# First mixer of a two-block kernel: queries projected ahead of the recurrence, near scores on row halves, modulation weights loaded in halves

## The chip, the cores and the metric

The kernel runs on one core of one Trainium2 chip. The number that counts is the device time of one execution in microseconds (us), lower is better. The engines that matter here are TensorE (PE), which multiplies matrices and loads its weights beside that (PEld); VectorE (DVE) and ScalarE (ACT), which work on elements; GpSimd (POOL); and SyncE (SP), whose queue issues the DMA transfers.

## The reference

Two transformer-like blocks, one after the other. The first has two layers, each with a mixer and a feed-forward part; every layer first turns the condition vectors into modulation rows (shift, scale, gate). This case touches only the first layer's mixer ("even mixer") and two thirds of that layer's modulation.

```python
m_lat = split((silu(c) @ mod_w[layer] + mod_b[layer]), 6)      # 1024 x 6144 weight, 2 rows (c, c_ctx)
h_lat = modulate(rms_norm(x), m_lat[0], m_lat[1])              # 512 tokens; h_ctx: 256 tokens
p  = split_parts(h_lat @ w_in)     # a_q 512, a_k 128, a_v 128, b_q, b_ff, b_fb, b_i, b_g 512 each
# attention: 8 query heads of 64 in 2 key heads; a 128-block sees its neighbours (window 128),
#            all 256 context keys and a sink column
q_lat = apply_rope(rms_norm(a_q));  k_lat = apply_rope(rms_norm(a_k))
s_lat = where(|k_pos - q_pos| <= 128, q_lat . k_lat * 64**-0.5, -inf);  s_ctx = q_lat . k_ctx * 64**-0.5
a_lat = softmax([sink, s_lat, s_ctx]) @ [v_lat, v_ctx]
# recurrence: 4 heads of 128, forward and backward, in chunks of 64, context first, then latent tokens
b_lat = rms_norm(gla(b_q, b_ff, b_i) + flip(gla(flip ...))) * silu(b_g)
y = concat(a_lat, b_lat) @ w_out                               # the same for the context tokens
```

## The kernel before

Tokens lie in columns, features in partitions: 512 latent and 256 context tokens, so one projection onto 128 features is done for 768 columns. Every weight matrix is loaded in float32 into a staging buffer `wr` (two buffers), split into a high part `wh` (ACT) and the rest `wl` (POOL) by `wsplit`, and used in three matmuls per 128 rows (`gemm`, L168 to L170): 8 x 3 matmuls of 128x512 (`hH`, `hL`, latent) and 8 x 3 of 128x256 (`cH`, `cL`, context). One projection is thus 48 matmuls, two PSUM tiles of the pool `mm`, which has two. Everything else that goes through PSUM in the mixer shares five banks with the tag `sm`.

`even_mixer` (its loop starts at `for hd in range(4)`) does four heads. Each head has, in this order in the code: the projections `wf`, `wb` (decays of the two directions), `wq`, `wg` (query and gate), the recurrence `hgrn_head`, which is a context part and then a latent part (each: scans and exponentials on DVE and ACT, transposes of `hkn` at L762, small matmuls at L778 to L812, a norm that ends in the matmul with `ones` at L823), then the attention queries' projection, their norm and rope (`qk_norm`, L627 to L635) and six attention blocks (`attend`: four latent blocks and two of context, scores at L649 and L652, transposes, values, and the last transposes at L701). PE fills what one head leaves open with projections of the next.

The order on each engine is not the order of the code: the tile framework sorts instructions by priority as they become ready and by the buffers that are free, once, at build time. On the chip each engine runs its list in that order.

Modulation of the layer is computed beside all this. Part 0 of its columns is done before the mixer; parts 1 and 2 (2048 columns each) are in a background list `bg` of Python generators, and `tick(1)` advances it by one step. A step is one row block of 128: a 1 MB load into the shared `wr` (L281), four matmuls of 32 columns each into column groups of one `sm` bank (L284), and an addition into `mrow` (L288, L290). In `two` (which does one projection) it is called as

```python
                self.later(100, self.tick, 1)
```

so it comes 100 priority steps behind the projection. Two matmul rows make one float32 matmul in the profile.

The keys of attention stand in two tiles `ak0`, `ak1` of 128 x 768. In each, one half of the partitions (64 rows, one key head) holds keys, and the other is zero, so that a product with the full 128-row query tile gives one key head's scores.

Of the kernel before, what the change touches and what calls it, by code (L numbers as in the profile page):

```python
# [67 lines left out]
class Core:  # L68
# [196 lines left out]
    def matvec(self, ps, sb, i0, w, c0, ncol, bias, dst, tag="mv"):  # L265


        nc, cond = self.nc, self.cond
        nj = ncol // 512
        np_ = 32 * nj  # L270
        rows = self.T(sb, [P, 512], "mrow")
        per = 2048 // ncol
        whole = tag == "mv"
        acc = None
        for k0 in range(0, KT, per):
            first, last = not whole or k0 == 0, not whole or k0 + per == KT
            if first:
                acc = self.T(ps, [P, 512], tag)
            r = self.wt("wr", [P, 2048])
            rv = r.rearrange("p (k c) -> p k c", k=per)  # L280
            nc.sync.dma_start(rv, w[k0 * P:(k0 + per) * P, c0:c0 + ncol].rearrange("(k p) c -> p k c", p=P))  # L281
            for kk in range(per):
                for j in range(nj):
                    nc.tensor.matmul(acc[32 * j:32 * j + 32, :], cond[:, k0 + kk, :], rv[:, kk, j * 512:(j + 1) * 512],  # L284
                                     start=(first and kk == 0), stop=(last and kk == per - 1), skip_group_check=True)
            if whole or k0 == 0:
                if last:
                    nc.vector.tensor_copy(rows[:np_, :], acc[:np_, :])  # L288
            else:
                nc.vector.tensor_tensor(rows[:np_, :], rows[:np_, :], acc[:np_, :], ALU.add)  # L290
            yield
        self.mv_out(ps, rows, nj, i0, 2, bias, dst, tag)

# [272 lines left out]
class Even(Core):  # L566
# [70 lines left out]
    def attend(self, ps, sb, q, k, vt, t, i, yq):  # L637
# [192 lines left out]
    def even_mixer(self, groups, ydram, side, mid, out):  # L830
# [3 lines left out]
        with tc.tile_pool(name="ev", bufs=1, reuse_waits="tile") as sb, tc.tile_pool(name="evmm", bufs=2, space=PSUM, reuse_waits="tile") as pm, \  # L834
# [33 lines left out]
            kr = self.T(sb, [P, TOK], "aq")  # L868
            self.qk_norm(ps, sb, pl, pc, self.qkg[:, 1:2], kr)

            k = [self.T(sb, [P, TOK], f"ak{i}") for i in range(2)]
            for i in range(2):
                rs, rz = slice(i * 64, i * 64 + 64), slice(64 - i * 64, 128 - i * 64)
                nc.gpsimd.memset(k[i][rz, :], 0.0)
                nc.gpsimd.tensor_copy(k[i][rs, :], kr[rs, :])
# [20 lines left out]
            for hd in range(4):  # L896
# [20 lines left out]

                r = self.wt("wr", [P, 2048])[:, :1024]
                rv = r.rearrange("p (k c) -> p k c", k=KT)
                for kv in range(2):  # L920
                    c = kv * 256 + hd * 64
                    nc.sync.dma_start(rv[:, :, kv * 64:(kv + 1) * 64], w[:, c:c + 64].rearrange("(k p) c -> p k c", p=P))
                H, L = self.wsplit(r)
                if hd == 3:
                    mid()
                pl, pc = two((H.rearrange("p (k c) -> p k c", k=KT), L.rearrange("p (k c) -> p k c", k=KT)))
                aq = self.T(sb, [P, TOK], "aq")
                self.qk_norm(ps, sb, pl, pc, self.qkg[:, 0:1], aq)
                yq = self.T(sb, [P, TOK], "yq", bufs=2)
                for i in range(6):  # L930
                    self.attend(ps, sb, aq, k, vt, hd, i, yq)
# [817 lines left out]
class Kernel(Second):  # L1749
    def run(self, out):  # L1750
# [13 lines left out]
        def matvecs(ps, sb, l, parts, tag="mv"):  # L1764
            for i in parts:
                c = slice(i * 16, i * 16 + 16)
                self.bg.append(self.matvec(ps, sb, 0, a["mod_w"][l], i * 2048, 2048,
                                           self.mb[:, l * 48 + i * 16:l * 48 + i * 16 + 16], self.modT[l][:, c, :], tag))
# [17 lines left out]
        with tc.tile_pool(name="x0", bufs=1, reuse_waits="tile") as xp, tc.tile_pool(name="n0", bufs=1, reuse_waits="tile") as sb, \  # L1786
# [9 lines left out]
            matvecs(*side(st, "mva"), 0, [0])  # L1796
# [26 lines left out]
        self.even_mixer(groups, yd, lambda ps, sb: matvecs(ps, sb, 0, [1, 2], "sm"), load_x, out_a)  # L1823
# [111 lines left out]
```

## Time and profile before

| what | us |
|---|---|
| time, median of 3 runs | 2943.16 (2942.12 to 2946.09) |
| time of the profiled execution | 2955.79 |
| its span in the trace | 2954.0 |
| PE busy in it | 2786.1 (94%) |
| DVE, ACT, POOL busy | 1396.0, 1064.5, 990.9 |
| mean granted TensorE clock | 0.972 of full speed |
| the four heads in the span | 127.6 to 610.6 |

The profiled execution is 12.6 us longer than the median of the timed runs. Positions below are microseconds from the start of the profiled span. The four heads take 16% of it. A head is read from its last attention transposes (L701) to those of the head before: 143.2, 116.1, 118.6 and 105.1 us.

### The profile page before, as it was taken

How to read it: one execution, taken by the hardware profiler on the slowest of the kernel's cores; microseconds unless marked ns; L12 is line 12 of the kernel's file. 1: busy time of each engine (PE TensorE's matmuls, PEld its weight loads, DVE VectorE, ACT ScalarE, POOL GpSimd, SP SyncE). 2: the span in 40 equal slices, each digit the busy share in tenths (PEclk: the TensorE clock that was granted, in tenths of full speed). 3: DMA queues.
4: the chain of work that ended last, by engine and by line, in shares of the span. 5: the costliest groups of instructions: out<-in, count | busy, mean ns of one | idle time of the engine just before them, and what ended most of it. 6: DMA issues, size and time to landing. Idle time of an engine off the chain costs nothing. (4 is left out here: it accounts for less than half of the span.)

```text
span 2954.0 us, 38203 instructions
## 1 busy us (share of the span) xinstructions
PE 2786.1 (94%) x15432; PEld 2301.8 (78%) x15432; DVE 1396.0 (47%) x2291; ACT 1064.5 (36%) x1964; POOL 990.9 (34%) x512
## 2 busy tenths in 40 slices
PE   5988989799999999999999999999999999999898
PEld 3866767678888888788888878877878788787677
DVE  5255655656645353633232326453363453542545
ACT  4234435433112112323233334222244444544533
POOL 2321212133223223234252435444434341332443
PEclk7999999999999999999999999999999999999999
DMA  6222121333323241122121214443124542443522
GB/s 258 72 84 85 49 84 54 97 106 117 106 106 127 82 157 40 54 71 85 57 86 57 72 47 168 161 151 101 57 98 139 159 147 74 126 131 128 191 77 86
DMA packets 216216, 306.39 MB, mean 104 GB/s; under 512 B 26918, under 2 KB 169800, under 8 KB 209512
## 3 DMA queue, kind: packets, MB, share of 16 engines
q1 hardware_dynamic: 216040, 303.96, 31.0%
q8 instruction: 121, 1.98, 0.3%
q14 instruction: 55, 0.45, 0.0%
HBM read 272.17 MB, written 31.75 MB: 103 GB/s over the span
## 5 line engine op out<-in xcount | busy, mean ns | idle before, releaser
L162 POOL TENSOR_TENSOR wl<-wr,wh 128x1024 fp32r<-128x1024 f32 x200 | 490.2, 2453 | 978.5 <-ACT wh L161 952.1
L168 PE MATMUL mm<-hH,wh 128*128 128x512 f32 (+1 forms) x1776 | 710.1, 401 | 13.3 <-ACT hH L189 5.0
L169 PE MATMUL mm<-hL,wh 128*128 128x512 f32 (+1 forms) x1776 | 707.8, 399 | 8.9 <-POOL hL L403 6.1
L170 PE MATMUL mm<-hH,wl 128*128 128x512 f32 (+1 forms) x1776 | 704.9, 397 | 2.5 <-POOL wl L162 2.5
L168 PEld LDWEIGHTS mm<-hH,wh 128*128 128x128 f32 x1776 | 338.5, 191 | 90.5 <-issue 7.2
L169 PEld LDWEIGHTS mm<-hL,wh 128*128 128x128 f32 x1776 | 339.0, 191 | 86.4 <-POOL hL L403 8.9
L161 ACT ACTIVATE wh<-wr 128x1024 fp32r<-128x1024 f32 x200 | 211.7, 1060 | 526.0 <-PE mm L169 427.0
L170 PEld LDWEIGHTS mm<-hH,wl 128*128 128x128 f32 x1776 | 339.3, 191 | 73.4 <-issue 3.7
L148 POOL TENSOR_TENSOR wl<-wr,wh 128x1024 fp32r<-128x1024 f32 x96 | 237.8, 2480 | 397.8 <-ACT wh L147 395.8
L416 DVE SCALAR_TENSOR_TENSOR x<-mm,modT,x 128x512 f32<-128x512 f32 (+1 forms) x340 | 213.9, 648 | 278.8 <-PE mm L170 276.4
L168 PE MATMUL mm<-aH,wh 128*128 128x512 f32 (+1 forms) x544 | 191.8, 354 | 3.0 <-DVE x L416 2.6
L169 PE MATMUL mm<-aL,wh 128*128 128x512 f32 (+1 forms) x544 | 191.0, 352 | 1.1 <-DVE aL L190 1.1
L170 PE MATMUL mm<-aH,wl 128*128 128x512 f32 (+1 forms) x544 | 191.7, 353 | 0.0
L168 PE MATMUL mm<-cH,wh 128*128 128x256 f32 x640 | 184.5, 288 | 6.5 <-DVE nt L398 6.3
L169 PE MATMUL mm<-cL,wh 128*128 128x256 f32 x640 | 185.0, 289 | 0.0
L170 PE MATMUL mm<-cH,wl 128*128 128x256 f32 x640 | 183.8, 287 | 0.0
L147 ACT ACTIVATE wh<-wr 128x1024 fp32r<-128x1024 f32 x96 | 101.1, 1055 | 165.7 <-PE mm L169 99.7
L168 PEld LDWEIGHTS mm<-cH,wh 128*128 128x128 f32 x640 | 123.4, 193 | 10.7 <-ACT cH L402 6.7
L169 PEld LDWEIGHTS mm<-cL,wh 128*128 128x128 f32 x640 | 123.4, 193 | 6.8 <-issue 4.4
L170 PEld LDWEIGHTS mm<-cH,wl 128*128 128x128 f32 x640 | 123.5, 193 | 2.8 <-issue 2.5
L190 DVE TENSOR_TENSOR aL<-sg,aH 128x512 fp32r<-128x512 f32 (+1 forms) x66 | 104.4, 1582 | 36.6 <-ACT aH L189 36.6
L314 DVE SCALAR_TENSOR_TENSOR macc<-wr,cond,macc 128x1024 f32<-128x1024 f32 (+1 forms) x56 | 109.8, 1979 | 18.6 <-DMA wr<-in_mod_w_dram 11.9
(504 smaller groups left out, 5060.5 us busy)
## 6 DMA issues: line engine op xcount, KB each, us to landing
wr<-in_mod_w_dram SPq DMA_DIRECT2D x48, 1024.0 KB, 5.3
wr<-in_ffn_w_in_dram SPq DMA_DIRECT2D x44, 1024.0 KB, 5.1
wr<-in_w_in_dram SPq DMA_DIRECT2D x36, 1024.0 KB, 5.4
wr<-in_odd_w_in_dram SPq DMA_DIRECT2D x24, 1024.0 KB, 5.1
wr<-in_ffn_w_out_dram SPq DMA_DIRECT2D x22, 1024.0 KB, 6.0
wr<-in_ada_w_dram SPq DMA_DIRECT2D x12, 1024.0 KB, 6.8
wr<-in_even_w_in_dram SPq DMA_DIRECT2D x18, 512.0 KB, 4.5
wr<-in_odd_w_out_dram SPq DMA_DIRECT2D x8, 1024.0 KB
```

The lines of the kernel that those rows point to most:

```text
L147: self.nc.scalar.activation(H, rv, AF.Copy)
L148: self.nc.gpsimd.tensor_tensor(L, rv, f32(H), ALU.subtract)
L161: self.nc.scalar.activation(H, v, AF.Copy)
L162: (engs[j] if engs else self.nc.gpsimd).tensor_tensor(L, v, f32(H), ALU.subtract)
L168: mm(out, lH, rH, start=first, stop=False, **kw)
L169: mm(out, lH, rL, start=False, stop=False, **kw)
L170: return mm(out, lL, rH, start=False, stop=last, **kw).ins.name
L190: (eng or self.nc.gpsimd).tensor_tensor(L, src, f32(H), ALU.subtract)
L314: nc.vector.scalar_tensor_tensor(acc[:, i, :], r[:, k, :], c, acc[:, i, :], ALU.mult, ALU.add)
L416: self.nc.vector.scalar_tensor_tensor(x, po, gate[:, m_:m_ + 1], x, ALU.mult, ALU.add)
```

## The change

Three parts. (a) In each head the attention queries' weight load, split, projection and `qk_norm` stand ahead of `hgrn_head` in the code; the gate tile `hg` has one buffer in place of two; `mid()` stands after `hst.close()`. (b) The keys are one tile `ak` of 128 x 768, both key heads below one another; only the 256 context keys are copied into two zero-padded tiles `akz0`, `akz1`. The near scores use 64 rows of queries and keys each, and both are issued before the mask products. (c) Modulation parts 1 and 2 go through a new function, `matvec_slow`: 16 loads of 128 x 1024 (512 KB) for a part, into one buffer `mwr` of their own, each issued a step before its use; a step is two matmuls of 32 columns and an addition on 64 rows. It is called at normal priority ahead of each of the two parts of a projection, so twice for one projection.

```diff
+    def matvec_slow(self, ps, sb, w, c0, bias, dst, tag):
+        nc = self.nc
+        rows = self.T(sb, [P, 512], "mrow")
+        before = None
+        for n in range(2 * KT + 1):
+            if before is not None:
+                r, k, h = before
+                acc = self.T(ps, [P, 512], tag)
+                for j in range(2):
+                    p0 = 64 * h + 32 * j
+                    nc.tensor.matmul(acc[p0:p0 + 32, :], self.cond[:, k, :], r[:, j * 512:(j + 1) * 512], start=True, stop=True,
+                                     skip_group_check=True)
+                hs = slice(64 * h, 64 * h + 64)
+                if k == 0:
+                    nc.vector.tensor_copy(rows[hs, :], acc[hs, :])
+                else:
+                    nc.vector.tensor_tensor(rows[hs, :], rows[hs, :], acc[hs, :], ALU.add)
+            if n < 2 * KT:
+                k, h = n // 2, n % 2
+                r = self.T(sb, [P, 1024], "mwr")
+                nc.sync.dma_start(r, w[k * P:(k + 1) * P, c0 + h * 1024:c0 + (h + 1) * 1024])
+                before = (r, k, h)
+            yield
+        self.mv_out(ps, rows, 4, 0, 2, bias, dst, tag)
...
-            nc.tensor.matmul(sB[:, kv * CTX:(kv + 1) * CTX], q[:, qs], k[kv][:, LAT:TOK], start=True, stop=True)
+            nc.tensor.matmul(sB[:, kv * CTX:(kv + 1) * CTX], q[:, qs], kz[kv], start=True, stop=True)
         if lat:
-            for s, kz in zip(sA, k):
-                nc.tensor.matmul(s[:, :n], q[:, qs], kz[:, js[0] * P:(js[-1] + 1) * P], start=True, stop=False)
+            for s, rs in zip(sA, kvs):
+                nc.tensor.matmul(s[:, :n], q[rs, qs], k[rs, js[0] * P:(js[-1] + 1) * P], start=True, stop=False)
+            for s in sA:
                 if i > 0:
...
             def two(wt):
-                self.later(100, self.tick, 1)
                 out = []
                 for g in groups:
+                    self.tick(1)
...
-                g = self.T(sh, [P, TOK], "hg", bufs=2)
+                g = self.T(sh, [P, TOK], "hg")
...
+                r = self.wt("wr", [P, 2048])[:, :1024]
+                rv = r.rearrange("p (k c) -> p k c", k=KT)
+                for kv in range(2):
+                    c = kv * 256 + hd * 64
+                    nc.sync.dma_start(rv[:, :, kv * 64:(kv + 1) * 64], w[:, c:c + 64].rearrange("(k p) c -> p k c", p=P))
+                H, L = self.wsplit(r)
+                pl, pc = two((H.rearrange("p (k c) -> p k c", k=KT), L.rearrange("p (k c) -> p k c", k=KT)))
+                aq = self.T(sb, [P, TOK], "aq")
+                self.qk_norm(ps, sb, pl, pc, self.qkg[:, 0:1], aq)
                 yq = self.T(sb, [P, TOK], "yq", bufs=2)
                 self.hgrn_head(ps, pso, sh, hd, q, g, kc, [None, None], v, yq)
...
-                r = self.wt("wr", [P, 2048])[:, :1024]
-                rv = r.rearrange("p (k c) -> p k c", k=KT)
...
-                H, L = self.wsplit(r)
-                if hd == 3:
                     mid()
-                pl, pc = two((H.rearrange("p (k c) -> p k c", k=KT), L.rearrange("p (k c) -> p k c", k=KT)))
-                aq = self.T(sb, [P, TOK], "aq")
-                self.qk_norm(ps, sb, pl, pc, self.qkg[:, 0:1], aq)
```

What this does to the built order, at three places. First PE in the second head. Before, from the end of the context part on: projections of the next head (`mm`) stand between the recurrence's own rows, right up to the transposes L762 that open the latent part.

```order
L169 MATMUL mm_2569<-cL_22_93,wh_447_2532 128x256
L170 MATMUL mm_2569<-cH_20_91,wl_448_2533 128x256
L168 MATMUL mm_2956<-hH_86,wh_541_2929 128x512
L169 MATMUL mm_2956<-hL_88,wh_541_2929 128x512
L170 MATMUL mm_2956<-hH_86,wl_542_2930 128x512
L168 MATMUL mm_2956<-hH_86,wh_541_2929 128x512
L169 MATMUL mm_2956<-hL_88,wh_541_2929 128x512
L170 MATMUL mm_2956<-hH_86,wl_542_2930 128x512
L168 MATMUL mm_2956<-hH_86,wh_541_2929 128x512
L169 MATMUL mm_2956<-hL_88,wh_541_2929 128x512
L762 MATMUL sm_2385<-ident_64,hkn_2369 128x128 x4
```

In the changed kernel, in the second head after the attention of the first: the steps of the modulation (L297, each from its own load of `mwr`), then the query norm (L645, L650), then the transposes of the recurrence's context part (L782). The lines shown are the end of nine steps in this place; between the first six stand 15, 23, 19, 18 and 19 projection matmuls.

```order
L168 MATMUL mm_3086<-cH_20_91,wh_560_2963 128x256
L169 MATMUL mm_3086<-cL_22_93,wh_560_2963 128x256
L170 MATMUL mm_3086<-cH_20_91,wl_561_2964 128x256
L297 MATMUL sm_2159<-mwr_2132,cond_76 32x512 x2
L297 MATMUL sm_2198<-mwr_2163,cond_76 32x512 x2
L348 MATMUL sm_2227<-ident_64,mrow_994 128x128 x4
L297 MATMUL sm_2276<-mwr_2234,cond_76 32x512 x2
L297 MATMUL sm_2307<-mwr_2280,cond_76 32x512 x2
L645 MATMUL sm_2343<-qsq_2340,sqc_453 128x512
L645 MATMUL sm_2350<-qsq_2340,sqc_453 128x256
L650 MATMUL sm_2355<-qraw_2339,sqc_453 128x512
L782 MATMUL sm_2382<-ident_64,hkn_2366 128x128 x2
```

What moved: before, no modulation step stands in this stretch without a projection next to it for long; now four steps end one after another, and from there to the latent part's small matmuls (60 rows on) there is no `mm` row. The third head has ten steps in this place, the last five of them one after another with six projection matmuls ahead of them; the fourth head has four.

Second, SP's queue in the same stretch of the changed kernel, from the store of the first head's recurrence on (`yd<-yq`).

```order
L944 DMA yd_82<-yq_1366 128x768
L935 DMA wr_597_3262<-in_even_w_in_dram 128x8x64 x2
L307 DMA mwr_1988<-in_mod_w_dram 128x1024
L953 DMA yd_82<-yq_1652 128x768
L307 DMA mwr_2019<-in_mod_w_dram 128x1024
L307 DMA mwr_2059<-in_mod_w_dram 128x1024
L878 DMA wr_756_3949<-in_even_w_in_dram 128x8x128
L307 DMA mwr_2090<-in_mod_w_dram 128x1024
L878 DMA wr_756_3949<-in_even_w_in_dram 128x8x128
L307 DMA mwr_2132<-in_mod_w_dram 128x1024
L878 DMA wr_761_3960<-in_even_w_in_dram 128x8x128
L307 DMA mwr_2163<-in_mod_w_dram 128x1024
```

What moved: before, this stretch had five 1 MB loads into `wr`; now there are nine loads of half that size, all into the one buffer `mwr`, with the weight loads of a later head and the store of the first head's attention between them.

Third, PE at the second attention block of the first head, changed kernel (`akz` are the padded context keys, `ak` the keys, `ay` a block's result).

```order
L667 MATMUL sm_1709<-akz_128_569,aq_1344 128x256
L718 MATMUL sm_1696<-avt_628,aPT_1683 128x64 x4
L667 MATMUL sm_1709<-akz_129_570,aq_1344 128x256
L671 MATMUL sm_1710<-ak_547,aq_1344 128x384
L721 MATMUL sm_1696<-ident_64,ay_1705 128x128
L671 MATMUL sm_1711<-ak_547,aq_1344 128x384
```

What moved: the two near scores (L671) have no mask product between them any more, but in blocks 1 and 2 of every head the full-width transpose L721 of the block before stands there; in blocks 0 and 3 they are neighbours.

## Rows read from the trace of the kernel before

**Rows 1.** The page, busy time of PE: us, share of the span, instructions.

```profile
PE 2786.1 (94%) x15432; PEld 2301.8 (78%) x15432; DVE 1396.0 (47%) x2291; ACT 1064.5 (36%) x1964; POOL 990.9 (34%) x512
```

**Rows 2.** Stretches of the second head: length, then busy time of PE, PEld, DVE, ACT, POOL, clock.

```profile
282.00:338.00 56.00, 47.00 (x363) 35.60 (x362) 36.71 (x64) 23.94 (x45) 19.46 (x10) 0.91 0.27 85
338.00:387.00 49.00, 47.75 (x294) 39.56 (x294) 26.85 (x79) 24.70 (x76) 6.50 (x4) 0.97 0.07 22
```

**Rows 3.** PE in order of time, first head: start, length, line, tiles.

```profile
127.61 0.40 PE L168 MATMUL mm<-hH,wh 128*128 128x512 f32 x1
...
135.80 1.04 PE L284 MATMUL sm<-wr,cond 128*32 128x512 f32 x2
137.09 1.04 PE L284 MATMUL sm<-wr,cond 128*32 128x512 f32 x2
...
139.37 0.50 PE L168 MATMUL mm<-hH,wh 128*128 128x512 f32 x1
...
164.26 0.44 PE L762 MATMUL sm<-ident,hkn 128*128 128x128 f32 x2
...
270.79 0.33 PE L701 MATMUL sm<-ident,ay 128*128 128x128 f32 x1
```

**Rows 4.** The same for heads two to four; idle time before in brackets.

```profile
282.04 0.44 PE L762 MATMUL sm<-ident,hkn 128*128 128x128 f32 x2
...
296.97 0.59 PE L823 MATMUL sm<-hcm,ones 128*128 128x256 f32 x2
...
307.00 0.63 PE L762 MATMUL sm<-ident,hkn 128*128 128x128 f32 x4 [2.53 <-DVE hkn L759]
...
327.02 1.56 PE L627 MATMUL sm<-qsq,sqc 128*128 128x512 f32 x4
...
338.18 1.94 PE L649 MATMUL sm<-ak,aq 128*128 128x256 f32 x4 [3.17 <-DVE aq L635]
...
386.86 0.33 PE L701 MATMUL sm<-ident,ay 128*128 128x128 f32 x1
...
505.45 0.33 PE L701 MATMUL sm<-ident,ay 128*128 128x128 f32 x1
...
610.56 0.33 PE L701 MATMUL sm<-ident,ay 128*128 128x128 f32 x1
```

**Rows 5.** PE and SP in order of time, modulation steps of the third head.

```profile
389.13 0.38 SPq L281 DMA_DIRECT2D wr<-in_mod_w_dram  x1
...
394.01 1.07 PE L284 MATMUL sm<-wr,cond 128*32 128x512 f32 x8 [2.40 <-DMA wr<-in_mod_w_dram]
397.36 1.89 PE L284 MATMUL sm<-wr,cond 128*32 128x512 f32 x2 [2.28 <-DMA wr<-in_mod_w_dram]
```

**Rows 6.** Line L281 (the 1 MB loads): PE's waits, us in all, times.

```profile
  PE sm L284: 7.0, 4
```

**Rows 7.** DMA issues at 389 and 227, then in 120 to 640: size, us to landing.

```profile
wr<-in_mod_w_dram SPq DMA_DIRECT2D x1, 1024.0 KB, 8.1
...
wr<-in_mod_w_dram SPq DMA_DIRECT2D x1, 1024.0 KB, 4.8
...
wr<-in_even_w_in_dram SPq DMA_DIRECT2D x12, 512.0 KB, 4.9
...
yd<-yq SPq DMA_DIRECT2D x6, 384.0 KB, 4.5
wr<-in_even_w_in_dram SPq DMA_DIRECT2D x8, 256.0 KB, 3.7
...
hH<-yd SPq DMA_DIRECT2D x4, 256.0 KB, 2.9
```

**Rows 8.** PE in order of time, a near score; then the 64-row matmuls of line L1512.

```profile
348.77 0.81 PE L652 MATMUL sm<-ak,aq 128*128 128x384 f32 x2
349.41 0.27 PE L701 MATMUL sm<-ident,ay 128*128 128x128 f32 x1
...
L1512 PE MATMUL sm<-dk,dq x96: 272/272/579, 2715.6 to 2832.7; 64*128 64x128 f32 x96
```

More of the change, by code (lines that the diff above doesn't have):

```diff
@@ L272, in matvec @@
         per = 2048 // ncol
-        whole = tag == "mv"
-        acc = None
+        acc = self.T(ps, [P, 512], tag)
         for k0 in range(0, KT, per):
-            first, last = not whole or k0 == 0, not whole or k0 + per == KT
-            if first:
-                acc = self.T(ps, [P, 512], tag)
             r = self.wt("wr", [P, 2048])
@@ L284, in matvec @@
                     nc.tensor.matmul(acc[32 * j:32 * j + 32, :], cond[:, k0 + kk, :], rv[:, kk, j * 512:(j + 1) * 512],
[L285 to L290, printed above, removed]
+                                     start=(k0 + kk == 0), stop=(k0 + kk == KT - 1), skip_group_check=True)
             yield
+        nc.vector.tensor_copy(rows[:np_, :], acc[:np_, :])
         self.mv_out(ps, rows, nj, i0, 2, bias, dst, tag)
+    def matvec_slow(self, ps, sb, w, c0, bias, dst, tag):
[5 more added lines that the diff above has]
+                r, k, h = before
+                acc = self.T(ps, [P, 512], tag)
+                for j in range(2):
[14 more added lines that the diff above has]
+        self.mv_out(ps, rows, 4, 0, 2, bias, dst, tag)
     def matvec_dve(self, ps, sb, i0, n, m, w, c0, bias, dst, tag):
@@ L635, in qk_norm, with attend @@
         nc.vector.tensor_tensor(out[:, :LAT], raw[:, :LAT], sq[:, :LAT], ALU.add)
-    def attend(self, ps, sb, q, k, vt, t, i, yq):
+    def attend(self, ps, sb, q, k, kz, vt, t, i, yq):
         nc = self.nc
@@ L867, in even_mixer @@
             pl, pc = two(wk)
-            kr = self.T(sb, [P, TOK], "aq")
-            self.qk_norm(ps, sb, pl, pc, self.qkg[:, 1:2], kr)
-            k = [self.T(sb, [P, TOK], f"ak{i}") for i in range(2)]
+            k = self.T(sb, [P, TOK], "ak")
+            self.qk_norm(ps, sb, pl, pc, self.qkg[:, 1:2], k)
+            kz = [self.T(sb, [P, CTX], f"akz{i}") for i in range(2)]
             for i in range(2):
                 rs, rz = slice(i * 64, i * 64 + 64), slice(64 - i * 64, 128 - i * 64)
-                nc.gpsimd.memset(k[i][rz, :], 0.0)
-                nc.gpsimd.tensor_copy(k[i][rs, :], kr[rs, :])
+                nc.gpsimd.memset(kz[i][rz, :], 0.0)
+                nc.gpsimd.tensor_copy(kz[i][rs, :], k[rs, LAT:])
             pl, pc = two(wv)
@@ L916, in even_mixer @@
                     hst.close()
-                r = self.wt("wr", [P, 2048])[:, :1024]
-                rv = r.rearrange("p (k c) -> p k c", k=KT)
-                for kv in range(2):
-                    c = kv * 256 + hd * 64
-                    nc.sync.dma_start(rv[:, :, kv * 64:(kv + 1) * 64], w[:, c:c + 64].rearrange("(k p) c -> p k c", p=P))
-                H, L = self.wsplit(r)
-                if hd == 3:
                     mid()
-                pl, pc = two((H.rearrange("p (k c) -> p k c", k=KT), L.rearrange("p (k c) -> p k c", k=KT)))
-                aq = self.T(sb, [P, TOK], "aq")
-                self.qk_norm(ps, sb, pl, pc, self.qkg[:, 0:1], aq)
                 yq = self.T(sb, [P, TOK], "yq", bufs=2)
                 for i in range(6):
-                    self.attend(ps, sb, aq, k, vt, hd, i, yq)
+                    self.attend(ps, sb, aq, k, kz, vt, hd, i, yq)
                 ys.append(yq)
@@ L1762, in mods, with matvec_at, slow @@
             return [self.affine(norm_g(l, n), self.modT[l], 3 * n, 3 * n + 1, i) for i in range(2)]
[L1764 to L1768, printed above, removed]
+        def matvec_at(i):
+            return a["mod_w"][0], i * 2048, self.mb[:, i * 16:i * 16 + 16], mod0[:, i * 16:i * 16 + 16, :]
+        def slow(ps, sb):
+            for i in (1, 2):
+                w, c0, bias, dst = matvec_at(i)
+                self.bg.append(self.matvec_slow(ps, sb, w, c0, bias, dst, "sm"))
         def norm_of(part, mod):
@@ L1795, in run @@
             self.load_tokens(ps, sb, groups, range(4, 6))
-            matvecs(*side(st, "mva"), 0, [0])
+            w, c0, bias, dst = matvec_at(0)
+            self.bg.append(self.matvec(*side(st, "mva"), 0, w, c0, 2048, bias, dst))
             self.tick(99)
@@ L1821, in out_a @@
             self.even_out_a(pm, groups, (self.hp, hcp), gates(mod0, 2), yd, ys)
-        self.even_mixer(groups, yd, lambda ps, sb: matvecs(ps, sb, 0, [1, 2], "sm"), load_x, out_a)
+        self.even_mixer(groups, yd, slow, load_x, out_a)
         self.norm_pool(xs)
```

## Prediction

> **What bounds the kernel now.** I began with the page: PE is busy for 94% of the span [rows 1], so the time is PE's list of work plus the holes in it. The stretches by time then say where holes are: in the second head PE is busy for 47.0 us of the 56 of the recurrence, and for 47.75 of the 49 of the attention [rows 2]. So attention is full, and anything that only fills it better gains nothing; the recurrence has room, because its own chain (DVE, ACT and small matmuls) is long and the projections of the next head are what PE does meanwhile. The order of time gives the stages. The second head runs from 270.79 to 386.86 [rows 3, 4], 116.1 us: modulation steps to 282.04 (11.3), context part to 296.97 (14.9), preparation of the latent part to 307.00 (10.0), latent part to 327.02 (20.0), query stage to 338.18 (11.2), attention (48.7). The third head, to 505.45, has 118.6; the fourth, to 610.56, 105.1 [rows 4]. The waits that a reader should see there: PE waits 2.53 for DVE's `hkn` at L762 and 3.17 for `aq` at L649 [rows 4], and 7.0 us in all, in four waits, for the 1 MB modulation loads [rows 6].
>
> Two prices come from these rows. A projection of 48 matmuls takes 135.80 - 127.61 = 8.19 us [rows 3]; counted in columns (24 of 512, 24 of 256) that is 0.228 and 0.114 us for one. A modulation step of two matmuls (first pair of rows) takes 137.09 - 135.80 = 1.29 with one wide projection matmul in it, so 1.06 [rows 3].
>
> **The change, part by part.**
>
> *First head.* Before, PE does three projections and three groups of modulation up to the first transposes at 164.26, 36.65 us from 127.61 [rows 3]. Now all five projections and nine two-matmul steps stand there: 5 x 8.19 + 9 x 1.06 = 50.5. Between two steps are 3 wide and 24 narrow projection matmuls (3.4 us) or 21 wide ones (4.8), so a step comes every 4.5 to 5.9 us, and loads that take about as long (below) cost a few tenths at most. After that, before, 106.5 us up to 270.79 with a query stage of its own of 11.2 (as in the second head) in them; that stage now lies ahead, beside the recurrence's own start, so 95.3. Sum 145.8 against 143.2: **+3**. Its bounds are 0 (the norm of the queries is hidden and more projections fit into holes) and +8 (240 projections of the second head fill it where some 170 did).
>
> *Second head, the modulation steps.* Here lies the case. `mwr` has one buffer, and the load for a step is issued when the matmul of the step before has read it. Nine steps follow one another, and PE's list puts the query norm and the recurrence behind them, so PE sits through each load. What a period costs is matmul, issue, landing and restart. The landing of 512 KB alone isn't in the trace: 256 KB took 2.9, and 1 MB without neighbours 4.8 [rows 7]. On the line between, 512 KB takes 3.5; the weight loads of 512 KB, in shorter pieces and two together, took 4.9, the upper end; 2.9 is the lower. Issue and restart: the load of 389.13 landed after 8.1 and PE began at 397.36 [rows 5, 7], 0.13 behind it; with as much on the issuing side, 0.25. So a period is 1.06 + 3.5 + 0.25 = 4.8 us (4.2 to 6.2). Fill is 15, 23, 19, 18 and 19 projection matmuls (3.4 to 3.6 us in the first four, 2.2 in the fifth), then nothing. After two waits of over 2 us in a row, one modulation matmul took 1.89 where it takes 1.04 [rows 3, 5], which is the lower of the two clock levels; so the three bare periods take 5.6. Five x 4.8 + 3 x 5.6 + the last matmul 1.9 + four transposes 0.7 = 43 us, where it was 11.3.
>
> *What follows it.* The query norm, context part and preparation had 14.9 + 10.0 + 11.2 = 36.1 before, with about 75 projection matmuls (12.8 us) between. Now they have none, since both `mm` banks hold results that wait for a buffer which the preparation frees. If every one of those matmuls had lain on the path, 23.3 is left; if none, 36.1. The chain there is DVE's and ACT's, and the query norm runs beside the context part now, so I take 25, with 20 and 31 as ends. The latent part takes 20.0 as before plus half a us (44 fillers against 43, two scans more in it, no modulation matmul): 20.5. Attention: 48.7, less two fillers (0.3), less one modulation matmul (1.0), less near scores (0.9): 46.5. Sum 43 + 25 + 20.5 + 46.5 = 135 against 116.1: **+19**.
>
> *Third head.* Ten steps; four periods are filled, one nearly and four not at all: 5 x 4.8 + 4 x 5.6 + 1.9 = 48. The rest as above: 48 + 25 + 20.5 + 46.5 = 140 against 118.6: **+21**.
>
> *Fourth head.* Four steps, three periods with 6, 0 and 11 matmuls, and transposes: 17. With 25, a latent part of 18 and 45.5 of attention that is 105.5 against 105.1: **0**. The attention's cover there is the output projection, which no longer fits in earlier; what is left over stands in the tail, at most 2 us.
>
> *Near scores.* One of 384 keys holds PE for 349.41 - 348.77 = 0.64 us [rows 8], one of 256 two thirds, 0.43; a head has four of each, 4.3 us. A 64-row matmul of 128 columns takes 0.272, as long as the full one of L701 above it (0.27), so half the rows alone gain nothing; only two that run at once do. No row shows two row halves at once. Bounds: nothing, or half of 4.3 x 4 heads = 8.6. Only the pairs of blocks 0 and 3 are neighbours; I take these as run together, 0.9 a head. The rule of the Trainium skill, "TensorE: Matmul & The Clock Gate", Part 3, is that small-row products on distinct row groups run concurrently; no run here shows it, and by it the pairs parted by L721 would stay single, which is the same 0.9.
>
> *Halved loads.* Loading the same bytes in twice as many transfers: 2 x 3.5 = 7.0 for what 4.8 did. The Trainium skill, "DMA: Bandwidth & Descriptors", section Bandwidth, says to batch transfers to 1 MiB or more, and "SBUF — State Buffer", on the setup-cost knee, gives 2 us and the bytes at 436 GB/s: 3.2 us for 512 KB and 4.4 for 1 MB, an estimate; the rows say 4.8 for the latter, so it is a little low. By it the sum would be 4 us smaller.
>
> *The rest.* The 7.0 us of waits for 1 MB loads [rows 6] are inside the old stage times that are replaced. `hg` with one buffer and `mid()` earlier delay nothing that I find late. SP's queue now has the first head's store (384 KB, 4.5 us [rows 7]) and 256 KB weight loads (3.7) between the modulation loads; what they add is in the upper end of the period.
>
> **Sum.** 3 + 19 + 21 + 0 = +43 us. The span of 2954.0 and its execution's 2955.79 stand 12.6 above the median; taking the same difference after, 2943.16 + 43 = **2986 us**.
>
> **Rivals.**
> - *The waits are used (other side).* While PE sits through the loads, DVE and ACT could finish the query norm and the recurrence's elementwise work, so that what follows the steps is only its small matmuls. If it took 10 in place of 25 in each of three heads, -45: -2 or, with every pair of near scores run together (8.6 in place of the 3.6 counted), -7: 2936. It decides where what follows falls under 11 us. For it: 43 us are long beside the 25. Against it: the steps' additions into `mrow` and the query norm stand in one DVE list, the additions first, so DVE waits with PE.
> - *Milder.* A period of 4.2, the bare ones 5.0, and 20 for what follows: the periods then gain some 9 us (0.6 in the twelve with little fill, 0.2 in the eight full ones), three heads 15: +19, 2962. For it: the landing of 2.9; the query norm beside the context part.
> - *Worse.* The store and the weight loads share the queues, periods 1.0 longer (20 of them, +20), or what follows takes 31 (+18): +61 to +81, 3004 to 3024. For it: 1 MB once took 8.1 beside a store [rows 7]; PE starts the context part at the low clock.
> - *No effect.* The chain is absorbed since DVE and ACT bound the head anyway. Against it: attention is 97% full, and PE has no work left there to catch up with.
>
> **How the numbers follow.** Chances: forecast (2970 to 3000) 0.57; milder (2952 to 2970) 0.14; worse (3000 to 3024) 0.18; the waits used 0.07; no effect 0.04. The range of 2952 to 3012 leaves out the last two and a part of the worse. Below 0.2% (6 us), a measurement of this kernel can't tell a change from none. Faster 0.07, same 0.05, slower 0.88; the forecast's own range is 2970 to 3000.
>
> **What would show it.** The new trace should have, between the first head's last attention transposes and the query norm of the second, nine pairs of matmuls with a wait for `mwr` ahead of the last four of about 3.5 us each; some 43 us there, 48 in the third head; no projection matmul from there to the latent part's small matmuls; and transfers of 512 KB landing in 3.5. It is wrong if landings are under 2.5, if the context part and the preparation go on while the steps wait, or if near scores gain over 8 us.

## The result, and the profile after

The changed kernel takes 3029.02 us (median of 4 runs, 3027.32 to 3034.27) where the kernel before takes 2943.46 beside it: ratio 1.0293, 95% interval 1.0275 to 1.0310, **+86 us, slower**. The direction was forecast; the size was twice the +43 of the forecast, and the time lies above its range (2952 to 3012) and above the worst rival (3024).

The stretches by time, as [rows 2] (length, then busy time and count of PE, PEld, DVE, ACT, POOL, then TensorE's granted clock, DMA share, GB/s). First the kernel before, from the first head's first projection to the output projection:

```profile
119.30:637.00 517.70, 461.68 (x3067) 358.57 (x3066) 281.07 (x612) 215.22 (x525) 120.28 (x69) 0.94 0.24 76
```

Then the changed kernel: the same stretch, and in the second head what follows the modulation steps, the latent part and the attention; last the fourth head's attention.

```profile
118.60:724.40 605.80, 493.46 (x3066) 362.10 (x3065) 275.14 (x628) 216.92 (x525) 118.23 (x69) 0.86 0.21 64
318.00:345.00 27.00, 13.71 (x80) 8.83 (x80) 16.59 (x36) 9.87 (x21) 4.49 (x4) 0.56 0.07 20
345.00:366.00 21.00, 20.93 (x195) 17.29 (x196) 14.48 (x26) 10.56 (x21) 5.87 (x2) 0.85 0.01 2
366.00:416.00 50.00, 47.55 (x298) 37.48 (x296) 27.11 (x79) 24.85 (x77) 9.15 (x6) 1.00 0.07 19
...
641.00:697.00 56.00, 52.15 (x281) 40.08 (x279) 26.23 (x75) 18.36 (x61) 5.14 (x6) 0.85 0.22 69
```

The two lines of the whole stretch hold most of the answer. The mixer is 605.8 - 517.7 = 88.1 us longer, which is all of the +86. PE is idle there for 605.8 - 493.5 = 112.3 us where it was for 56.0: **+56 of waiting**. And the same number of matmul records (3066 and 3067) takes 493.5 us of busy time in place of 461.7: **+32 of longer matmuls**, at a mean granted clock of 0.86 in place of 0.94. In the stretch 318 to 345 PE is busy for half of the time, and the clock is 0.56, near the lower of the two levels (1.2 of 2.4 GHz).

PE in order of time, second head, as [rows 4, 5]: the last four of nine modulation steps, the query norm, the transposes that open the latent part, and the start and end of the attention; then the same places of heads three and four.

```profile
297.34 1.05 PE L297 MATMUL sm<-mwr,cond 128*32 128x512 f32 x4 [1.57 <-DMA mwr<-in_mod_w_dram]
304.70 1.92 PE L297 MATMUL sm<-mwr,cond 128*32 128x512 f32 x4 [6.31 <-DMA mwr<-in_mod_w_dram]
...
310.31 1.92 PE L297 MATMUL sm<-mwr,cond 128*32 128x512 f32 x4 [1.79 <-DMA mwr<-in_mod_w_dram]
316.01 1.92 PE L297 MATMUL sm<-mwr,cond 128*32 128x512 f32 x4 [3.77 <-DMA mwr<-in_mod_w_dram]
317.86 2.85 PE L645 MATMUL sm<-qsq,sqc 128*128 128x512 f32 x4
...
345.07 1.08 PE L782 MATMUL sm<-ident,hkn 128*128 128x128 f32 x4 [6.98 <-DVE hkn L779]
...
365.94 1.03 PE L667 MATMUL sm<-akz,aq 128*128 128x256 f32 x4
...
416.23 0.33 PE L721 MATMUL sm<-ident,ay 128*128 128x128 f32 x1
...
470.12 2.93 PE L645 MATMUL sm<-qsq,sqc 128*128 128x512 f32 x4
...
498.38 1.09 PE L782 MATMUL sm<-ident,hkn 128*128 128x128 f32 x4 [6.97 <-DVE hkn L779]
...
518.54 1.03 PE L667 MATMUL sm<-akz,aq 128*128 128x256 f32 x4
...
570.63 0.48 PE L721 MATMUL sm<-ident,ay 128*128 128x128 f32 x1
...
593.04 1.24 PE L645 MATMUL sm<-qsq,sqc 128*128 128x512 f32 x3
...
619.32 1.09 PE L782 MATMUL sm<-ident,hkn 128*128 128x128 f32 x4 [7.25 <-DVE hkn L779]
...
640.97 1.03 PE L667 MATMUL sm<-akz,aq 128*128 128x256 f32 x4
...
696.92 0.27 PE L721 MATMUL sm<-ident,ay 128*128 128x128 f32 x1
```

The reader sees a step of 1.05 us turn into one of 1.92 after a wait of 6.31, and what stands behind it stay slow: the transposes at 345.07, for which PE has waited 6.98 for DVE with no projection to do, take 1.08 where four took 0.63 before [rows 4]. The waits of PE over the mixer (us in all, times, longest):

```profile
PE sm L297 <- DMA mwr<-in_mod_w_dram: 47.7, 19, 6.3
PE sm L782 <- DVE hkn L779: 25.7, 6, 7.3
PE ho L818 <- DVE hsT L805: 17.7, 10, 3.6
PE sm L709 <- ACT aP L692: 8.4, 4, 3.0
```

Before, the loads of modulation made it wait 7.0 [rows 6], and `aq` 13.5, which is gone now. The other three were:

```profile
PE sm L762 <- DVE hkn L759: 14.5, 6, 4.5
PE ho L798 <- DVE hsT L785: 3.4, 5, 1.0
PE sm L689 <- ACT aP L672: 1.6, 4, 0.6
```

How long the new loads took from issue to landing (min, median, max):

```profile
DMA to landing us min/median/max: 3.5/3.8/5.2
```

### The profile page after: what moved, and what is told of

Its sections match the earlier page's. It is cut to its first block, busy times and chain, and to the rows that moved or that the text cites. A ratio compares the mean times of both kernels' runs of the same rounds, so it can differ in the third digit from the quotient of the medians.

```text
span 3025.5 us, 38295 instructions
## 1 busy us (share of the span) xinstructions
PE 2805.9 (93%) x15432; PEld 2296.5 (76%) x15432; DVE 1391.8 (46%) x2307; ACT 1065.8 (35%) x1964; POOL 988.2 (33%) x512
## 5 line engine op out<-in xcount | busy, mean ns | idle before, releaser
L190 POOL TENSOR_TENSOR wl<-wr,wh 128x1024 fp32r<-128x1024 f32 (+2 forms) x40 | 73.6, 1845 | 160.8 <-ACT wh L189 142.5
```

What stands on the lines that cost most here:

```text
L190: (eng or self.nc.gpsimd).tensor_tensor(L, src, f32(H), ALU.subtract)
```

## The experiments

Two theories. L: the loads into the one buffer are the cause, by the waits, by the place the steps take from the projections, and by the slow matmuls after. Q: moving the queries takes cover from the recurrence and the attention. Medians stand beside runs of the kernel before on the same chip (2943.5 to 2946.8); differences go by the ratios. "Mixer" is the stretch from the first head's first projection to the output projection.

**e1, the change without its third part.** Against the full change; the code is cut to the calls, and the modulation's functions are those of the kernel before.

```diff
+                self.later(100, self.tick, 1)
                 out = []
                 for g in groups:
-                    self.tick(1)
...
-        self.even_mixer(groups, yd, slow, load_x, out_a)
+        self.even_mixer(groups, yd, lambda ps, sb: matvecs(ps, sb, 0, [1, 2], "sm"), load_x, out_a)
```

> The change without its third part: queries moved and row halves, but modulation as before (1 MB loads in the shared buffers, one step per projection, 100 priorities behind). Theory L (the modulation steps wait for loads in the one buffer, and their list takes the projections away from the recurrence): nearly all of the +86 us is gone, time within -10 to +15 us of before. Rival Q (moving the queries takes the cover off the recurrence and the attention): at least half of it stays, +40 to +80.

Measured 2986.19, ratio 1.0143 (1.0129 to 1.0157): +42. That is Q's number, at its lower end: half of the change's cost stays without any half load.

**e2, row halves alone.**

```diff
-            for s, kz in zip(sA, k):
-                nc.tensor.matmul(s[:, :n], q[:, qs], kz[:, js[0] * P:(js[-1] + 1) * P], start=True, stop=False)
+            for s, rs in zip(sA, kvs):
+                nc.tensor.matmul(s[:, :n], q[rs, qs], k[rs, js[0] * P:(js[-1] + 1) * P], start=True, stop=False)
+            for s in sA:
```

> The kernel before with the near scores on row halves alone. By the rows of the changed kernel a pair of neighbours takes 0.64 us where it took 0.98, and a single one of 384 keys 0.84 where it took 0.64: two gains of 0.34 and four losses of 0.2 in a head cancel, 0 to -3 us in all. If pairs that run at once counted in full as I forecast, -4. A rival in which row halves cost in every head would show +5 or more.

Measured 2948.64, ratio 1.0015 (1.0006 to 1.0024): +4, a small loss, between my 0 to -3 and the rival's +5. Rows of the changed kernel, from its first head and the last one from its fourth, say why there is no gain:

```profile
222.38 1.03 PE L667 MATMUL sm<-akz,aq 128*128 128x256 f32 x4
223.34 0.70 PE L671 MATMUL sm<-ak,aq 64*128 64x256 f32 x4
223.97 0.28 PE L676 MATMUL sm<-maskb,identb 128*128 128x128 bf16 x2
...
233.28 0.91 PE L671 MATMUL sm<-ak,aq 64*128 64x384 f32 x2
234.12 0.33 PE L721 MATMUL sm<-ident,ay 128*128 128x128 f32 x1
...
667.02 0.92 PE L671 MATMUL sm<-ak,aq 64*128 64x384 f32 x4
```

Two full-height products of 256 keys hold PE for 223.34 - 222.38 = 0.96 us, two row halves side by side for 0.63. But a single half between full-height rows holds it for 234.12 - 233.28 = 0.84 where the full one of 384 keys took 0.64 [rows 8]. Two pairs gain 0.33 each in a head, four singles lose 0.20 each. The row at 667.02, two halves of 384 keys side by side, held PE until 667.87, 0.85: the second half costs nothing, but one half alone costs as much as the two. (In the fourth head the pairs are blocks 0 and 2, not 0 and 3 as the built order was read above. In e2 itself pairs and singles stand at still other blocks.) The Trainium skill, "TensorE: Matmul & The Clock Gate", Part 3, has distinct row groups run at once; the rows agree, with 0.85 for two halves where one takes 0.84, and 0.63 against 0.96. That a lone half is dearer than a full product I had not expected.

**e3, moved queries alone.**

```diff
+                self.qk_norm(ps, sb, pl, pc, self.qkg[:, 0:1], aq)
                 yq = self.T(sb, [P, TOK], "yq", bufs=2)
                 self.hgrn_head(ps, pso, sh, hd, q, g, kc, [None, None], v, yq)
...
-                self.qk_norm(ps, sb, pl, pc, self.qkg[:, 0:1], aq)
```

> The kernel before with the queries alone moved ahead of the recurrence (gate tile in two buffers). Theory L: within -10 to +15 us, since the order keeps projections between the rows of the recurrence. Rival Q: +40 to +80. The built order shows no projection in the last two of six attention blocks, so 2 to 5 us a head may come back as waits for the softmax.

Measured 2970.11, ratio 1.0089 (1.0074 to 1.0103): +26. Between the two theories, above L's range and below Q's. Waits of PE over its mixer:

```profile
PE ho L798 <- DVE hsT L785: 12.2, 12, 2.9
PE sm L689 <- ACT aP L672: 11.6, 8, 2.9
PE mm L168 <- ACT wh L147: 7.6, 3, 4.2
```

The wait for `aq` (13.5) is gone, but `hsT` went from 3.4 to 12.2, `aP` from 1.6 to 11.6, and 7.6 are new, for the split of the query weights, which come through the shared `wr` behind the modulation loads. The +26 here and the +4 of e2 leave 12 of e1's 42; e1 also has the gate tile in one buffer, and no run changes that alone, so whether the 12 are that or the two parts together stays open.

**e4, row halves and halved loads, queries not moved** (gate tile in one buffer; the halved loads alone were not run). Against the full change:

```diff
-                self.qk_norm(ps, sb, pl, pc, self.qkg[:, 0:1], aq)
                 yq = self.T(sb, [P, TOK], "yq", bufs=2)
                 self.hgrn_head(ps, pso, sh, hd, q, g, kc, [None, None], v, yq)
...
+                self.qk_norm(ps, sb, pl, pc, self.qkg[:, 0:1], aq)
```

> Row halves and modulation in halves, queries where they were (gate tile in one buffer). Theory L: +60 to +90, since the steps stand between the heads as in the full change. Rival Q: below +40.

Measured 3003.76, ratio 1.0204 (1.0188 to 1.0220): +60. That is L's number, at its lower end. So with queries unmoved, halved loads (and the one gate buffer) cost some 55 over e2; on top of moved queries and row halves (e1) they cost 44. Both theories hold a part.

**e5, the full change, loads taken away.**

```diff
-                r = self.T(sb, [P, 1024], "mwr")
-                nc.sync.dma_start(r, w[k * P:(k + 1) * P, c0 + h * 1024:c0 + (h + 1) * 1024])
+                if n == 0:
+                    r = self.T(sb, [P, 1024], "mwr")
+                    nc.sync.dma_start(r, w[1 * P:2 * P, c0:c0 + 1024])
```

> The full change, but each part of the modulation loads its first half block once and uses it in all 16 steps (so modulation parts 1 and 2 are computed from the wrong weights; same matmuls and additions). No step waits for a load. Theory L (the loads are the cause, through PE's waits, the place that the steps take from projections, and the low clock after the waits): +86 falls to between -10 and +15 us. Rival Q (queries moved ahead are a cost of their own): +25 to +45 stays, as in the runs with queries moved and 1 MB loads (+26, +42).

Measured 2930.51, ratio 0.9946 (0.9925 to 0.9966): **-16**, beyond L's range on the fast side. The full change, with the same matmuls and additions, is faster than before once no step waits for a load: 102 us hang on the loads. Its mixer, and in the second head what follows the steps:

```profile
120.30:624.20 503.90, 459.71 (x3066) 356.24 (x3065) 284.72 (x628) 216.47 (x525) 121.44 (x69) 0.93 0.15 45
279.60:306.70 27.10, 23.13 (x166) 18.67 (x163) 18.81 (x38) 13.25 (x26) 7.81 (x6) 0.94 0.14 40
```

Idle 44.2 (of 112.3) and busy 459.7 (of 493.5): the longer matmuls go away with the waits. The order is another too. In the second head, from the query norm to the transposes that open the latent part, the changed kernel has no projection matmul and this one 81. PE's rows at the end of the steps:

```order
L297 MATMUL sm_2246<-mwr_2204,cond_76 32x512 x2
L297 MATMUL sm_2275<-mwr_2204,cond_76 32x512 x2
L646 MATMUL sm_2309<-qsq_2306,sqc_453 128x512
L646 MATMUL sm_2316<-qsq_2306,sqc_453 128x256
L168 MATMUL mm_2948<-hH_86,wh_541_2925 128x512
L169 MATMUL mm_2948<-hL_88,wh_541_2925 128x512
L170 MATMUL mm_2948<-hH_86,wl_542_2926 128x512
```

So the list at build time is part of the cost: where steps wait for loads, it puts the projections between the steps, and they are used up when the recurrence comes. The recurrence is hardly longer for that: this stretch takes 27.1 us with 81 projection matmuls in it at a clock of 0.94, and 27.0 without any at 0.56 in the changed kernel (25.2 and 28.3 in the third head, 24.1 and 26.3 in the fourth). What is lost is the 81, which here add next to no time and there stand among the steps.

The steps' own stretches, from the last attention transposes of a head to the query norm of the next, hold as much as the whole difference. Sums over heads two to four: length and PE's busy time, then the same with the modulation's matmuls (L297) alone; first the changed kernel, then e5.

```profile
sum 122.10, PE 74.52 PEld 38.33 DVE 16.94 ACT 12.26 POOL 10.78; mean PE 24.84 PEld 12.78 DVE 5.65 ACT 4.08 POOL 3.59
sum 122.10, PE 32.44 PEld 4.15; mean PE 10.81 PEld 1.38
...
sum 19.33, PE 17.40 PEld 7.27 DVE 13.97 ACT 2.39 POOL 1.65; mean PE 5.80 PEld 2.42 DVE 4.66 ACT 0.80 POOL 0.55
sum 19.33, PE 11.40 PEld 2.66; mean PE 3.80 PEld 0.89
```

Of the 103 us between 122.1 and 19.3, some 46 are PE's idle time (47.6 and 1.9), some 36 projection matmuls (205 in place of 19, with a few transposes), and 21 the modulation's own matmuls, which in the changed kernel stand two by two and in part at the low clock.

**e6 and e7, without modulation parts 1 and 2**: the kernel before, and queries moved with row halves.

```diff
             for i in parts:
                 c = slice(i * 16, i * 16 + 16)
+                if tag == "sm":
+                    nc.vector.memset(self.modT[l][:, c, :], 0.5)
+                    continue
                 self.bg.append(self.matvec(ps, sb, 0, a["mod_w"][l], i * 2048, 2048,
```

> The kernel before without modulation parts 1 and 2 (their rows are filled with 0.5: 16 MB of loads, 128 matmul rows and the additions left out). PE spends 32 us on them in the mixer and waits 7 for their loads: -30 to -45 us. It is the base for the next.

> Queries moved and row halves, gate tile in two buffers, modulation parts 1 and 2 left out in the same way. Theory L: moved queries cost only by what they do to the modulation steps and their loads, so this is as fast as the kernel before without modulation or up to 15 us faster (13.5 us of waits for the query norm are gone): -35 to -60 against before. Rival Q: some 26 us slower than that one, -5 to -20 against before.

Measured 2872.97, ratio 0.9752 (0.9739 to 0.9765), -73, and 2894.76, ratio 0.9825 (0.9810 to 0.9840), -52. The first is far beyond my -30 to -45: modulation costs more here than its matmuls and waits. The second lies in L's range against the kernel before only for that reason; against e6, its base, it is 22 us slower where L had it equal or faster. So moved queries and row halves cost 22 us with no modulation in the mixer at all: the rival Q, and my theory's account of e3 falls. Where: first head and last head of e6, then of e7 (with what is behind the last head up to the output projection), and one from the middle of each.

```profile
119.00:251.80 132.80, 125.46 (x861) 105.01 (x860) 69.53 (x156) 69.79 (x161) 45.05 (x24) 0.97 0.15 44
251.80:346.50 94.70, 89.44 (x657) 73.40 (x656) 58.78 (x139) 49.52 (x125) 23.11 (x15) 0.98 0.12 37
...
441.30:565.00 123.70, 109.95 (x760) 90.99 (x759) 70.59 (x159) 46.67 (x118) 27.74 (x18) 0.94 0.27 81
```

```profile
119.60:262.20 142.60, 134.97 (x905) 111.47 (x905) 73.58 (x156) 73.25 (x166) 46.40 (x25) 0.98 0.16 44
262.20:358.20 96.00, 90.25 (x662) 72.34 (x661) 61.84 (x140) 50.09 (x125) 24.40 (x15) 0.98 0.12 37
...
454.10:584.60 130.50, 109.61 (x702) 88.01 (x701) 64.07 (x155) 40.69 (x104) 23.71 (x17) 0.87 0.19 59
```

A middle head costs the same (94.7 and 96.0). The first head has 44 more records and takes 9.8 longer; the last has 58 fewer and takes 6.8 longer all the same: with its projections done ahead it has fewer to cover its recurrence (24 projection matmuls in the context part and its preparation, none from there to the attention, where e6 has 49 and 35), and its mean granted clock is 0.87. Each head does its queries a stage earlier, so one projection less is left for the last head, which has no next head to borrow from. The last head's attention says the same of the changed kernel: it is as long there (640.97 to 696.92) as in e5 (first line) and in e7 (second line).

```profile
540.77:596.67 55.90, 52.05 (x279) 39.94 (x278) 26.32 (x75) 18.36 (x61) 5.14 (x6) 0.85 0.22 71
501.13:557.10 55.97, 52.10 (x280) 40.07 (x279) 26.30 (x75) 18.36 (x61) 5.14 (x6) 0.85 0.22 69
```

**e8, one edit on the kernel before.**

```diff
-                self.later(100, self.tick, 1)
+                self.tick(1)
```

> The kernel before with one edit: the modulation step of 1 MB is called at normal priority ahead of a projection, not 100 priorities behind. In the built order its four matmuls now stand together everywhere; before, in the first head, projections stood between them, 3.6 us for what takes 1.0 when together, in four places. If that is PE time on the path: -8 to -12 us, faster than before. If the loads are now late at these places, as in the full change: 0 to +15.

Measured 2922.43, ratio 0.9920 (0.9908 to 0.9932): **-24 us, faster than both kernels**, twice what I expected of it. A step of four matmuls now stands together (first line; the second is the mixer):

```profile
127.15 1.07 PE L284 MATMUL sm<-wr,cond 128*32 128x512 f32 x8 [1.51 <-DMA wr<-in_mod_w_dram]
...
119.80:615.10 495.30, 444.10 (x3067) 351.69 (x3066) 271.05 (x612) 215.46 (x525) 119.39 (x69) 0.94 0.25 79
```

Before, the first step there ran from 135.80 to 139.37 [rows 3]. The mixer is 495.3 long in place of 517.7: PE's busy time falls by 17.6, to 444.1, and its idle time by 4.9. The steps' own matmuls are 12 us of that (22.1 of busy time in place of 34.2): four that stand together, on four column groups, take 1.07, where one alone takes 1.04 [rows 3] and a step of two in the changed kernel 1.05. So tearing a step apart, or halving it, makes PE pay for it twice or more. The 12 are what I expected; no run shows where the other 12 come from.

**e9 and e10, half loads called ahead of the attention blocks** (e9 without moved queries, e10 the full change).

```diff
-                    self.tick(1)
...
                 for i in range(6):
+                    self.tick(2)
                     self.attend(ps, sb, aq, k, kz, vt, hd, i, yq)
```

> Row halves and modulation in halves with its own buffer, queries where they were, and the two calls of a step made ahead of each attention block in place of ahead of each part of a projection. Same 32 loads, same buffer. In the built order the steps of the first head are apart by 12 to 35 projection matmuls all through the attention. Theory L: a step's load (3.8 us) is then hidden by attention, where it was not between the heads; half of the later heads still lose their cover in the context part. +60 (the run with row halves and halves between the heads) falls to -25 to +15. Rival (halves in one buffer are slow wherever they stand): +40 or more.

> The full change with the calls of a step moved in the same way ahead of the attention blocks. Theory L: +86 falls by 50 or more, to 0 to +35, above the run before by the price of moved queries (20 to 25 us). Rival: +70 or more.

Measured 2985.30, ratio 1.0138 (1.0123 to 1.0153), +41, and 3009.16, ratio 1.0213 (1.0196 to 1.0230), +63. Some 30% of the cost goes (60 to 41, 86 to 63), far less than L's numbers: e9 lies in its rival's range, e10 between the two. Waits of PE in the mixer of e10:

```profile
PE sm L782 <- DVE hkn L779: 26.5, 6, 8.0
PE sm L709 <- ACT aP L692: 18.0, 9, 3.5
PE sm L297 <- DMA mwr<-in_mod_w_dram: 7.8, 8, 3.7
```

The waits for loads fall from 47.7 to 7.8, as meant, but the recurrence still waits for DVE as long as in the changed kernel (`hkn` 25.7 there), and `aP` is up by 10. The projections are used up in the attention now, and the recurrence is as bare. PE's wait for the loads is thus not all that the loads cost. That the cover used up is what remains here I read from the order; no run shows it alone.

**e11, e1 with whole steps at normal priority** (and the gate tile in two buffers).

```diff
-                self.later(100, self.tick, 1)
+                self.tick(1)
```

> Queries moved and row halves, modulation in 1 MB steps as before, but called at normal priority ahead of a projection (the edit that gave -24 us on the kernel before). If moved queries cost a fixed 20 to 25 us and whole steps gain 24, they add: -10 to +10. If the moved queries are what makes steps and query weights meet between the heads, the gain is lost: +20 to +40.

Measured 2969.46, ratio 1.0086 (1.0071 to 1.0101): +25. Against e1, whole steps gain 17, though e11 has the gate tile in two buffers and e1 in one; moved queries and row halves cost 49 on top of e8, more than the 22 that they cost alone. The number is the second reading's and not the sum's; that steps and query weights meet is not shown by it.

**e12, quarter loads in two own buffers.**

```diff
-        for n in range(2 * KT + 1):
+        for n in range(4 * KT + 1):
...
-                r = self.T(sb, [P, 1024], "mwr")
+                r = self.T(sb, [P, 512], "mwr", bufs=2)
```

> The full change with two own buffers of half the size: 64 loads of 256 KB, one matmul for a step, four calls for a projection. Two loads are then on the way at once. Theory L with the single buffer as the cause: PE's 48 us of waits for mwr fall to 15 to 30, time +50 to +70. If what counts is the place of the steps and the bytes behind each other, waits stay at 40 or more: +75 to +95.

Measured 3018.23, ratio 1.0245 (1.0230 to 1.0260): +72, just above L's range. PE's waits for the loads:

```profile
PE sm L296 <- DMA mwr<-in_mod_w_dram: 18.6, 13, 5.0
```

The waits for loads fall by 29 as L had it for the single buffer, and the time by 14. The rest is about what single matmuls cost that no longer run in pairs: those of the modulation keep PE busy for 62.6 us (windows of that line over the mixer), where they took 45.5 in the changed kernel and 34.2 before.

## Why the prediction was right in direction and wrong in size

- **A step waits for its load, and the period.** Right. 512 KB landed in 3.8 us (forecast 3.5), and the bare period from 310.31 to 316.01 is 5.7 (forecast 5.6). Where weight loads were in the queue, one took 7.4 (297.34 to 304.70): there a weight load ahead of it in SP's queue waited for its `wr` buffer, and the step's own load was issued at 299.73, 1.3 us after the matmul that had read `mwr` ended. The steps took 46, 54 and 22 us in heads two to four, where the terms were 43, 48 and 17: 14 us too little in all, most of it the weight loads, which I had put in the upper end of the range only. The price of a step, 1.06, is right by luck: the rows that it came from show one matmul of 32 columns (two rows make one) and beside it a narrow projection matmul, not a wide one. Two take 1.05 because column groups run side by side (e8).
- **What follows, bare of projections.** Right in kind: 27, 28 and 26 us where 25 was taken, 7 too little in all. PE waits 6.98 for `hkn` in one piece. With projections in it, it is 24 to 27 us long (e5), so losing them made it little longer.
- **First head.** +2.0 where +3 was said, by luck. I counted from the second projection (127.61) before, but all five after, and the first of them begins at 118.6: one projection (8.2) too many. The stretch up to the first transposes (177.99) took 59.4 where it took 45.0 from 119.3, +14.4; with four projections my terms would have given +5.7. So some 9 us in it, among them 1.9 of waits, were not in the sum.
- **Fourth head: the step that failed.** I had 105.5 against 105.1, "0". It takes 126.3 (570.63 to 696.92), +21. Its attention alone takes 55.95 where 45.5 was taken, and its latent part 21.7 for 18; the other 7 are its steps and what follows them. The sum spoke of the output projection as cover and did not price that the head had lost its own. That price, some 14 us against the sum, has nothing to do with the loads: the attention takes 55.9 with no step waiting for a load (e5) and 56.0 without modulation parts 1 and 2 (e7). Against e6, which has the queries where they were, it is 6.8 us for e7's last head.
- **Attention: the other failed step.** Terms of 46.5, 46.5 and 45.5 measured 50.3, 52.1 and 56.0: 20 us, near half of the miss, 10.5 of them those of the fourth head. I took it as full and let it become shorter by near scores and matmuls moved out. It did not, and the loads are not why: in e5 it takes 51.7, 56.9 and 55.9. It waits for `aP` (8.4 in all, from 1.6), and the 0.9 a head of near scores did not come (e2).
- **The clock.** I had 0.8 us more for each bare step. All of the mixer's 3066 records together took 32 us longer, and the low level lasted through the context part (0.56 in 318 to 345), not only through the steps. But that is not 32 us on the path: 11 of them are modulation matmuls (45.5 for 34.2), of which a part is the halving, and what follows the steps takes 27.0 at 0.56 and 27.1 at 0.94 (e5). In the stages the rest is inside the numbers above; how much of it the clock alone lengthens no run shows.
- **The profiled execution.** It stood 12.6 above the median, and I kept that distance. After, the profiled one has the shortest time of its four; behind the mixer it takes 2301.1 us, the one of before 2317.0. Only the mixer tells of the change: +88 there, +86 in the medians.
- **The rival on the other side** (waits are used by DVE and ACT) has no support: what follows the steps never fell under 26 us in the changed kernel. The worse rival was nearest: its +20 for longer periods measured 14, its +18 for what follows 7; the attention and the fourth head were in no rival.

What the parts cost together, from the runs: moved queries and row halves 22 without modulation (e7 against e6). Modulation parts 1 and 2 then add 138 in the changed kernel (+86 against -52 of e7, with the gate tile in one buffer), 73 in the kernel before (e6), 49 in whole steps (-24 against -73), and 36 in the full change if no step waits for a load (-16 against -52). The halved loads cost 44 over e1 and 55 over e2; moved queries cost 26 over e4, and with the row halves 42 by themselves (e1). By the order in which one takes the change apart, the loads are half of it or somewhat more. The way in which they cost is for the most part not PE's wait at the step. Of the 102 us between the changed kernel and e5, some 46 are that wait, some 36 projections that the recurrence would have covered, and 21 the modulation's matmuls, longer two by two and at the low clock; how these last two share the 21 stays open. Also open is why moved queries cost 49 on top of e8 and 22 alone.

## What to carry to other kernels

When a list is sorted at build time, a step that waits for a load doesn't only wait: it draws the independent matmuls to itself, and the serial part that used to cover them is left bare. That part took 24 to 27 us here with them and 26 to 28 without: what is lost is not its length but the work that it hid. So price a new wait with the work that it draws to itself (36 us here, beside 46 of waiting), and count the last round of a loop, which has no next round to borrow work from. And look for steps that are torn apart by interleaving: one priority was worth 24 us here, 12 of them by the steps' own matmuls, where the whole change cost 86.

## What the runs showed of the hardware that was not expected

A single 64-row fp32 product among full-height ones held TensorE 0.84 us for 384 columns, and two side by side 0.85; a full one held it 0.64. For 256 columns two halves side by side held it 0.63, two full ones 0.96. Products of 32 columns on different column groups ran side by side: one held TensorE about 1.04 us, two 1.05, four 1.07. The granted clock stayed at 0.56 for a 27 us stretch in which PE was busy for half of the time, and was back at 1.00 in the attention that followed; between them, in 345 to 366, PE was busy for 20.93 of 21 us and the mean was 0.85.
